# Weight sums of a Strassen down projection: 32 subtractions on GpSimd instead of VectorE

## The chip, the cores and the metric

The kernel runs on one NeuronCore of a Trainium2 chip. A core has a matrix engine (TensorE, PE in the profile; its weight loads are PEld) and three engines for elementwise work: VectorE (DVE), ScalarE (ACT) and GpSimd (POOL). SyncE (SP) only issues DMAs here. Each engine takes its instructions in its own order, and semaphores join them. The metric is the time of one execution on the device in microseconds, the median of several runs.

## The reference, cut to what matters

One decoder layer on 256 tokens (T = 256 in the kernel) with D = 1024 and a feed-forward width FF of 2816: a half-weighted feed-forward block, a mixer of two branches, and a second half-weighted feed-forward block. All numbers are float32.

```
def swiglu(x, w_gate, w_up, w_down):
    return (jax.nn.silu(x @ w_gate) * (x @ w_up)) @ w_down

h = h + 0.5 * rmsnorm(swiglu(rmsnorm(h, ffn1_pre_g[l]), ffn1_w_gate[l], ffn1_w_up[l], ffn1_w_down[l]), ffn1_post_g[l])
...
h = h + rmsnorm(merged @ w_out[l], mix_post_g[l])
h = h + 0.5 * rmsnorm(swiglu(rmsnorm(h, ffn2_pre_g[l]), ffn2_w_gate[l], ffn2_w_up[l], ffn2_w_down[l]), ffn2_post_g[l])
```

The change touches only `@ w_down`, in both feed-forward blocks, called f1 and f2 in the kernel.

## The kernel before

**Split weights.** A float32 product is made of three products of reduced-precision parts: high by high, low by high, high by low. So each piece of a weight that comes from DRAM (`raw`) is split into a high part by ScalarE (`whi`, `wqh`: a cast, L355, L132, L157) and a low part by VectorE (`wlo`, `wql`: the piece minus its high part, L356, L138, L158). TensorE can use a piece when both parts are there. A low part of 128x1024 elements reads two operands in SBUF.

**A feed-forward block.** Gate and up go in 11 chunks of 256 columns (j = 0 to 10; `pg_f` and `pup_f` are their results in PSUM, L437). ScalarE and VectorE evict them (L443, L444: VectorE reads one operand from PSUM), form the product `sg_f` (L1100) and split it into `gh_f` and `gl_f` (L416, L417). In the trace and below, chunk numbers count weight pieces: two to each j.

**Down by Strassen.** Four of the five 512-row groups of `w_down` are multiplied as Strassen quads: seven products in place of eight, each on a sum or a quarter of the weights. The plan `DOWN` is "q1 Q2 q3 Q0 ppp": quads 1 and 3 form their weight sums on the spot (`wt`, L124), quads 2 and 0 use sums that were made ahead and stand in DRAM (`sums_f`), and three plain pieces end the stage.

**The sums that are made ahead.** While gate and up run, `stored_sums` (L208 to L230) makes them, in four jobs per block: two halves (kt = 0, 1) of quad 2, then two of quad 0. A job loads two 128x1024 tiles of the weights (`ws`, L217), forms four differences of 128x512 in place (L222, L224, L227, L229), and stores each tile when it is ready (L225, L230). Loads and stores are DMAs that GpSimd issues. After its first load, GpSimd copies one element a partition of the tile (L219, `landed`), which keeps it from issuing more until that load has landed. SyncE loads the stored sums again in the down stage (`raw` from `sums_f`).

**What sets the order.** `store_sums` in the block's loop over j steps the jobs: the place in the program is written by hand. During gate and up a scheduler with a cost model arranges the instructions of each engine; from the down stage on the order is the written one. `ws`, `whi`, `wlo`, `wqh`, `wql`, `wt`, `gh_f` and `gl_f` take turns in one pool of 29 equal buffers (`k4`). A new tile gets the buffer that comes free first by that model, and its first writer waits until the last reader or writer of the old one is done. A `ws` buffer is free once its store has landed.

Of the kernel before, what the change touches and what calls it, by code (L numbers as in the profile page):

```python
# [56 lines left out]
def tile_hybrid_layer(ctx: ExitStack, tc: tile.TileContext, x, ffn1_pre_g, ffn1_w_gate, ffn1_w_up,  # L57
# [4 lines left out]
    nc = tc.nc  # L62
# [5 lines left out]
    def k4(shape, name, dt=F32):  # L68
        return sb.tile(shape, dt, tag="k4", name=name, bufs=K4_BUFS)
# [10 lines left out]
    def tiny(n, name):  # L80
        return sb.tile([P, n], F32, tag=f"tiny{n}", name=name, bufs=10 if n > 4 else 16)
# [129 lines left out]
    def stored_sums(w, k0, store, kt):  # L211

        t = []
        for i in range(2):
            t.append(k4([P, 2, 512], f"ws{k0}{kt}{i}"))
            rows = slice(k0 + (2 * i + kt) * P, k0 + (2 * i + kt + 1) * P)
            nc.gpsimd.dma_start(t[i], w[rows, :].rearrange("p (q c) -> p q c", q=2))  # L217
            if i == 0:
                nc.gpsimd.tensor_copy(tiny(2, f"landed{k0}{kt}")[:, 0:1], t[i][:, 0, 0:1])  # L219
            yield  # L220
        (q0, q1), (q2, q3) = ((x_[:, 0], x_[:, 1]) for x_ in t)
        nc.vector.tensor_sub(q0, q1, q0)  # L222
        yield
        nc.vector.tensor_sub(q1, q3, q1)  # L224
        nc.gpsimd.dma_start(store[:, 0, kt, :], t[0].rearrange("p q c -> p (q c)"))  # L225
        yield
        nc.vector.tensor_sub(q3, q3, q0)  # L227
        yield
        nc.vector.tensor_sub(q2, q2, q3)  # L229
        nc.gpsimd.dma_start(store[:, 1, kt, :], t[1].rearrange("p q c -> p (q c)"))  # L230
        yield

# [815 lines left out]
    def ffn(post_v, tag, ready, turned, then, products):  # L1048
# [29 lines left out]
        then()  # L1078
        sums = {}
        jobs = [stored_sums(*job) for job in stored.get(tag, ())]  # L1080

        def store_sums(at):
# [814 lines left out]
```

## Time and profile before

| | us |
|---|---|
| median of 3 runs | 725.26 (725.09 to 725.95) |
| profiled execution, first to last instruction (span) | 724.0 |
| weight sums on VectorE, busy | 22 (32 instructions) |
| GpSimd busy in the whole span | 57.5 |

The profile is one execution of its own, known by its span of 724.0 us; the runs also count what lies around the span, and their median is 1.26 us above it. In a row of the timeline stand the start, the duration, the engine, the line, the operation, the output and inputs, their shape, and in brackets how long the engine sat idle before it and what released it. A row "x3" joins three neighbours. In a row of groups stand the busy time, the mean in ns of one, and idle time ahead. A row of windows gives for a stretch of time its length and the busy time of PE, PEld, DVE, ACT and POOL, the granted clock, and the share and rate of the DMAs. Instructions of one engine overlap a little, so the step from start to start is shorter than the duration.

### The profile page before, as it was taken

To read this page: it belongs to the slowest core of one execution; us is meant where nothing else is said; L and a number is where in the kernel's file an instruction comes from. 1 tells how busy PE (TensorE), PEld (TensorE's weight loads), DVE (VectorE), ACT (ScalarE), POOL (GpSimd) and SP (SyncE) were. 2 spreads that over 40 slices of the span, in tenths; PEclk is the share of its full clock that TensorE was granted. 3 is DMA by queue.
4 is the path that set the end of the run, shared out by engine and by line. 5 is a ranking of instruction groups with operands and counts; after the bars stand their busy time and mean duration, and the time that the engine had idled before them with its cause. 6 is when DMAs were issued, how large, how long until landed. Compare 5 with 4: busy or idle time off the path is not lost.

```text
span 724.0 us, 10650 instructions
## 1 busy us (share of the span) xinstructions
PE 716.8 (99%) x3959; PEld 615.1 (85%) x3959; DVE 642.9 (89%) x993; ACT 487.1 (67%) x828; POOL 57.5 (8%) x103
## 2 busy tenths in 40 slices
PE   9999999999999999999999999999999999999996
PEld 7888898888878888899888788888888888888885
DVE  6889999999979999887996998789786899989996
ACT  5666666767767676879965577775664676577572
POOL 4401110000200000000000000000011021200000
PEclk9999999999999999999999999999999999999998
DMA  8969977877673657666564663464454868876851
GB/s 300 273 200 333 319 250 285 321 270 280 184 231 119 183 167 234 205 210 196 153 226 148 205 221 130 169 234 163 163 169 145 280 215 311 290 273 268 312 204 58
DMA packets 100213, 161.01 MB, mean 222 GB/s; under 512 B 3309, under 2 KB 69441, under 8 KB 99137
## 3 DMA queue, kind: packets, MB, share of 16 engines
q1 hardware_dynamic: 92880, 135.80, 56.7%
q0 software_dynamic: 6976, 24.00, 9.3%
q8 instruction: 31, 0.51, 0.3%
q10 hardware_dynamic: 304, 0.53, 0.2%
q14 instruction: 22, 0.17, 0.1%
HBM read 150.85 MB, written 9.47 MB: 221 GB/s over the span
## 4 chain that ended last, share of the span: by engine, by line
PE 99%; DVE 0%; DVEq 0%; ACT 0%; issue 0%; ACTq 0%
PE pup_f L437 14%; PE pg_f L437 14%; PE pxs L437 6%; PE pws L478 6%; PE pgt L478 6%; PE acc_f2p L934 5%; PE acc_f1p L934 5%; PE pbc L437 3%; PE pk L437 3%; PE pq L437 3%; PE pn_f L494 3%; PE pn_mx L478 3%; PE pwd L478 3%; PE pn_f L478 3%; PE pz L437 2%; PE acc_f1p L772 2%
## 5 line engine op out<-in xcount | busy, mean ns | idle before, releaser
L356 DVE TENSOR_TENSOR wlo<-raw,whi 128x1024 fp32r<-128x1024 f32 x204 | 243.5, 1221 | 17.1 <-ACT whi L355 16.6
L355 ACT CAST whi<-raw 128x1024 fp32r<-128x1024 f32 x204 | 206.9, 1050 | 11.1 <-DMA raw<-in_w_in_dram 4.0
L437 PE MATMUL pg_f<-u_f,whi 128*128 128x512 f32 x288 | 69.0, 390 | 0.0
L437 PE MATMUL pup_f<-u_f,whi 128*128 128x512 f32 x288 | 68.7, 391 | 0.0
L437 PEld LDWEIGHTS pg_f<-u_f,whi 128*128 128x128 f32 x288 | 53.9, 188 | 11.1
L437 PEld LDWEIGHTS pup_f<-u_f,whi 128*128 128x128 f32 x288 | 52.9, 188 | 10.2
L437 PEld LDWEIGHTS pg_f<-u_f,wlo 128*128 128x128 f32 x288 | 36.9, 191 | 1.4
L437 PE MATMUL pup_f<-u_f,wlo 128*128 128x256 f32 x288 | 37.5, 283 | 0.0
L437 PE MATMUL pg_f<-u_f,wlo 128*128 128x256 f32 x288 | 37.4, 283 | 0.0
L437 PEld LDWEIGHTS pup_f<-u_f,wlo 128*128 128x128 f32 x288 | 35.9, 192 | 0.0
L158 DVE TENSOR_TENSOR wql<-raw,wqh 128x1024 fp32r<-128x1024 f32 x28 | 32.9, 1222 | 0.9 <-ACT wqh L157 0.9
L478 PE MATMUL pgt<-whi,u_mx 128*128 128x512 f32 x128 | 33.1, 393 | 0.0
L416 ACT CAST gh_f<-sg_f 128x512 fp32r<-128x512 f32 x18 | 11.2, 621 | 30.3 <-DVE sg_f L1100 26.3
L437 PE MATMUL pxs<-u_mx,whi 128*128 128x512 f32 x128 | 29.9, 390 | 0.0
L443 ACT COPY su_f<-pup_f 128x256 f32<-128x256 f32 x36 | 13.4, 372 | 24.1 <-PE pup_f L437 24.1
L478 PEld LDWEIGHTS pgt<-whi,u_mx 128*128 128x128 f32 x128 | 23.6, 188 | 5.3 <-issue 0.7
L437 PEld LDWEIGHTS pxs<-u_mx,whi 128*128 128x128 f32 x128 | 23.8, 188 | 4.8
L157 ACT CAST wqh<-raw 128x1024 fp32r<-128x1024 f32 x28 | 27.4, 1048 | 0.0
L132 ACT CAST wqh<-wt 128x1024 fp32r<-128x1024 f32 x16 | 16.8, 1053 | 15.2 <-DVE wt L124 11.5
L1397 DVE SCALAR_TENSOR_TENSOR xs<-xr,cols_b,xs 128x255 f32<-128x255 f32 (+2 forms) x48 | 21.2, 480 | 0.8 <-ACT xs L1394 0.6
L1471 DVE TENSOR_TENSOR E<-E,cbm 128x768 f32<-128x768 f32 x16 | 15.3, 958 | 6.0 <-ACT E L511 6.0
L511 ACT ACTIVATE s<-s,nm 128x128 f32<-128x128 f32 (+1 forms) x32 | 14.3, 447 | 9.3 <-DVE nm L1564 7.2
(492 smaller groups left out, 1700.5 us busy)
## 6 DMA issues: line engine op xcount, KB each, us to landing
raw<-in_w_in_dram SPq DMA_DIRECT2D x40, 1024.0 KB, 5.2
raw<-in_ffn_w_gate_dram SPq DMA_DIRECT2D x20, 1024.0 KB, 5.8
raw<-in_ffn_w_up_dram SPq DMA_DIRECT2D x20, 1024.0 KB, 5.6
raw<-in_ffn_w_down_dram SPq DMA_DIRECT2D x18, 1024.0 KB, 5.3
ws<-in_ffn_w_down_dram POOLq DMA_DIRECT2D x16, 512.0 KB, 6.3
sums_f<-ws POOLq DMA_DIRECT2D x16, 512.0 KB, 5.5
raw<-sums_f SPq DMA_DIRECT2D x8, 1024.0 KB, 7.0
raw<-in_ssd_w_branch_dram SPq DMA_DIRECT2D x8, 1024.0 KB, 5.0
```

Of the source, the lines that this page charges most:

```text
L132: nc.scalar.copy(hi, src)
L157: nc.scalar.copy(hi, src)
L158: nc.vector.tensor_sub(lo, src, hi.bitcast(F32))
L355: last_cast[0] = behind(nc.scalar.copy(hi, r[:, js, :]), "cast").ins
L356: m = nc.vector.tensor_sub(lo, r[:, js, :], hi.bitcast(F32))
L437: nc.tensor.matmul(to, w_(j)[:, m * P:(m + 1) * P], x_(j), start=first and j == 0, stop=not first and j == KD - 1, skip_group_check=True)
L478: nc.tensor.matmul(acc, a(k0 + j), b(j), start=first and i == 0, stop=last and i == 11)
L494: nc.tensor.matmul(accs[b], x_(k0 + j), w_(j), start=first and j == 0 and w_ is wh and x_ is acts[b][0], stop=last and j == 3 and w_ is wl)
L772: nc.tensor.matmul(acc[b][q][:, cs] if to is None else to, x_[:, ts], w_(kt)[:, halves[q]][:, cs], start=to is not None and kt == 0 and x_ ...
L934: nc.tensor.matmul(bank[p], x_, w_, start=p not in begun, stop=last and p in (1, 5, 6, 7))
L1397: nc.vector.scalar_tensor_tensor(dst[:, m, s:], acc[:, m, :T - s], cw(3 - s, c), dst[:, m, s:], ALU.mult, ALU.add)
L1471: nc.vector.tensor_tensor(E, E, cbm[g].unsqueeze(1).to_broadcast([P, 2, 3 * P]), ALU.mult)
```

## The change

The four differences of a job are computed by GpSimd. Nothing else in the text of the kernel changes.

```
         (q0, q1), (q2, q3) = ((x_[:, 0], x_[:, 1]) for x_ in t)
-        nc.vector.tensor_sub(q0, q1, q0)
+        nc.gpsimd.tensor_sub(q0, q1, q0)
         yield
-        nc.vector.tensor_sub(q1, q3, q1)
+        nc.gpsimd.tensor_sub(q1, q3, q1)
         nc.gpsimd.dma_start(store[:, 0, kt, :], t[0].rearrange("p q c -> p (q c)"))
         yield
-        nc.vector.tensor_sub(q3, q3, q0)
+        nc.gpsimd.tensor_sub(q3, q3, q0)
         yield
-        nc.vector.tensor_sub(q2, q2, q3)
+        nc.gpsimd.tensor_sub(q2, q2, q3)
         nc.gpsimd.dma_start(store[:, 1, kt, :], t[1].rearrange("p q c -> p (q c)"))
```

TensorE and SyncE keep their instructions in the same order. GpSimd has 32 more (138 for 106), VectorE 32 fewer, and the scheduler arranges some others anew.

On GpSimd's queue, in gate and up of f1, this is the end of the first job and the begin of the second (`ws_448` and `ws_513` are the first job's tiles, `ws_630` and `ws_743` the second's; + stands only after the change, - only before):

```order
+L227 TENSOR_TENSOR ws_513<-ws_513,ws_448 128x512
+L229 TENSOR_TENSOR ws_513<-ws_513 128x512
+L230 DMA sums_f_66<-ws_513 128x1024
 L217 DMA ws_630<-in_ffn_w_down_dram 128x1024
 L219 COPY landed_632<-ws_630 128x1
-L230 DMA sums_f_66<-ws_513 128x1024
+L222 TENSOR_TENSOR ws_630<-ws_630 128x512
 L217 DMA ws_743<-in_ffn_w_down_dram 128x1024
+L224 TENSOR_TENSOR ws_630<-ws_743,ws_630 128x512
 L225 DMA sums_f_66<-ws_630 128x1024
```

The first load of the second job stood ahead of the first job's last store, and now stands behind it. The second load of a job now stands behind a subtraction.

On VectorE, at the end of gate and up of f1, these rows stood around the first low parts of quad 1 before (`wql221`, `wql222`, `wql223`; `ws011_1200` is the second tile of the last job; in brackets the semaphores that a row waits for, where DMAHW are loads by SyncE, DMASW DMAs by GpSimd, and Pool GpSimd's instructions):

```order
L138 TENSOR_TENSOR wql221_1310<-raw22_1155,wqh221_1308 128x1024 [waits DMAHW0_49]
L227 TENSOR_TENSOR ws011_1200<-ws011_1200,ws010_1087 128x512 [waits DVE_49]
L229 TENSOR_TENSOR ws011_1200<-ws011_1200 128x512 [waits DVE_49]
L444 TENSOR_TENSOR su_f19_1253<-pup_f191_1265,su_f19_1253 128x256 [waits Activation_49]
L138 TENSOR_TENSOR wql222_1314<-raw23_1211,wqh222_1312 128x1024 [waits DMAHW1_49]
L1100 TENSOR_TENSOR sg_f19_1202<-su_f19_1253,sg_f19_1202 128x512 [waits DVE_49]
L124 TENSOR_TENSOR wt225_1318<-raw22_1155 128x1024 [waits DMASW3_49]
L417 TENSOR_TENSOR gl_f18_1092<-sg_f19_1202,gh_f18_1091 128x512 [waits Activation_49]
L138 TENSOR_TENSOR wql223_1320<-raw23_1211,wqh223_1316 128x1024 [waits PE_49]
```

And after the change, at the same place:

```order
L138 TENSOR_TENSOR wql221_1310<-raw22_1155,wqh221_1308 128x1024 [waits DMAHW0_49,PE_49,Activation_49]
L444 TENSOR_TENSOR su_f19_1253<-pup_f190_1264,su_f19_1253 128x256 [waits Activation_49]
L138 TENSOR_TENSOR wql222_1314<-raw23_1211,wqh222_1312 128x1024 [waits DMASW3_49,DMASW1_49,DMAHW1_49,Activation_49,Pool_49]
L444 TENSOR_TENSOR su_f19_1253<-pup_f191_1265,su_f19_1253 128x256 [waits Activation_49]
L124 TENSOR_TENSOR wt225_1318<-raw22_1155 128x1024 [waits DMASW4_49,DMASW6_49,DMASW2_49,DMASW0_49]
L1100 TENSOR_TENSOR sg_f19_1202<-su_f19_1253,sg_f19_1202 128x512 [waits DVE_49]
L138 TENSOR_TENSOR wql223_1320<-raw23_1211,wqh223_1316 128x1024 [waits DMASW2_49,DMASW4_49,Activation_49,Pool_49]
```

The subtractions are gone from VectorE's order, `gl_f` has moved behind the third low part, and the buffers are dealt anew: `wql222` takes one that the last job's first tile held, `wql223` the one of its second tile, so they wait for that job's stores (L225 and L230). Before, neither of them waited for a DMA of GpSimd. The same rows stand in f2.

## The prediction

> **What bounds the kernel now.** I read the page first (busy time per engine, the granted clock, the chain that ended last), then the waits of TensorE, then the chain through the first feed-forward stage.
>
> ```profile
> PE 716.8 (99%) x3959; PEld 615.1 (85%) x3959; DVE 642.9 (89%) x993; ACT 487.1 (67%) x828; POOL 57.5 (8%) x103
> PEclk9999999999999999999999999999999999999998
> PE 99%; DVE 0%; DVEq 0%; ACT 0%; issue 0%; ACTq 0%
> PE warm L571 <- DVE zeros L551: 1.1, 1, 1.1
> 115.03 5.57 PE pup_f L437 x32
> 120.60 5.54 PE pg_f L437 x32
> ...
> 131.71 38.08 PE acc_f1p L934 x168
> ...
> 663.47 38.08 PE acc_f2p L934 x168
> ```
>
> TensorE is busy for 716.8 of 724.0 us at an undisturbed clock. Its only wait in the whole program is 1.1 us before its first instruction. In the chain each row begins where the one before ends: 115.03 + 5.57 is 120.60, and so on into the down stage at 131.71. The first part of the down stage takes 38.08 us in both FFNs. So TensorE sets the time from the first matmul to the last, and the end is a short tail behind it that the change does not touch. An engine that is relieved beside it gives TensorE nothing to gain; an engine that falls behind can cost one for one. The question is only whether the change makes something late.
>
> **What the change removes.** Thirty-two subtractions leave VectorE.
>
> ```profile
> L229 DVE TENSOR_TENSOR ws<-ws 128x512 f32<-128x512 f32 x8 | 5.5, 689 | 0.1
> L222 DVE TENSOR_TENSOR ws<-ws 128x512 f32<-128x512 f32 x8 | 5.5, 687 | 0.0
> L224 DVE TENSOR_TENSOR ws<-ws,ws 128x512 f32<-128x512 f32 x8 | 5.5, 686 | 0.0
> L227 DVE TENSOR_TENSOR ws<-ws,ws 128x512 f32<-128x512 f32 x8 | 5.5, 686 | 0.0
> ...
> 118.33 0.69 DVE L224 TENSOR_TENSOR ws<-ws,ws 128x512 f32<-128x512 f32 x1
> ...
> 120.70 0.69 DVE L227 TENSOR_TENSOR ws<-ws,ws 128x512 f32<-128x512 f32 x1
> 121.42 0.69 DVE L229 TENSOR_TENSOR ws<-ws 128x512 f32<-128x512 f32 x1
> 122.03 0.42 DVE L444 TENSOR_TENSOR su_f<-pup_f,su_f 128x256 f32<-128x256 f32 x1
> 122.37 1.22 DVE L138 TENSOR_TENSOR wql<-raw,wqh 128x1024 fp32r<-128x1024 f32 x1
> ...
> 125.84 1.23 DVE L138 TENSOR_TENSOR wql<-raw,wqh 128x1024 fp32r<-128x1024 f32 x1
> ```
>
> The groups sum to 4 x 5.5 = 22 us of busy time. Each holds VectorE's line for about 0.60 us, because neighbouring instructions overlap (121.42 to 122.03), so VectorE gains 32 x 0.60 = 19.2 us, half in each FFN. Three of these subtractions stand just ahead of the second and third low part (wql) of the first down quad, so those could come 1.8 us sooner. By the first part, none of this shortens TensorE's work: I count the relief at **0**, with at most 0.4 us for small stalls that the modelled ends of matmuls hide.
>
> **What it adds on GpSimd.** No subtraction of this size on GpSimd is in the trace. The nearest rows:
>
> ```profile
> L1308 POOL TENSOR_SCALAR_AFFINE_SELECT dneg<-dneg 128x256 f32<-128x256 f32 x1 | 0.4, 415 | 0.0
> L554 POOL TENSOR_SCALAR_AFFINE_SELECT ident<-ident 128x128 f32<-128x128 f32 x1 | 0.3, 285 | 0.0
> L219 POOL COPY landed<-ws 128x1 f32<-128x1 f32 x8 | 9.7, 1213 | 38.2 <-DMA ws<-in_ffn_w_down_dram 38.2
> ```
>
> From 128 to 256 elements the select grows by 415 - 285 = 130 ns, about 1.02 ns an element, over a base of 155 ns. With one pass over 512 elements that gives 0.155 + 512 x 1.02 ns = 0.68 us, the low end; with the two operands read one after the other, 0.155 + 1024 x 1.02 ns = 1.20 us, the high end. I take 1.2, since the subtraction reads two operands and no row shows GpSimd reading two at the price of one. Gain is excluded here, as nothing else goes from GpSimd.
>
> The Trainium skill, "GPSIMD Engine Reference", section 3.1, has a two-input add of 2048 fp32 elements at 4497 ns against 2293 ns on VectorE; scaled to 512 elements that would be an estimate of some 1.1 us, and the sum with it would be the same.
>
> **The job on GpSimd's queue.** The four subtractions of a job now stand between its DMAs, so a job runs one step after another. Two queue rows give the pieces, with the landing times of the DMA table:
>
> ```profile
> 25.12 0.53 POOL L217 DMA_DIRECT2D ws<-in_ffn_w_down_dram  x1
> 32.77 0.19 POOL L219 COPY landed<-ws 128x1 f32<-128x1 f32 x1 [7.12 <-DMA ws<-in_ffn_w_down_dram]
> ...
> 122.41 0.54 POOL L230 DMA_DIRECT2D sums_f<-ws  x1 [2.56 <-DVE ws L229]
> ...
> ws<-in_ffn_w_down_dram POOLq DMA_DIRECT2D x16, 512.0 KB, 6.3
> sums_f<-ws POOLq DMA_DIRECT2D x16, 512.0 KB, 5.5
> ```
>
> First load to landed 7.65, the copy 0.19, second load 6.3, two stores to issue 1.08: 15.2 us, and four subtractions of 1.2 make 20.0. Four jobs from 25.12 on would end at 105.1, without waits for VectorE. Each of the 20 reads by GpSimd (16 subtractions, 4 copies) can also wait for VectorE, as the copies do now: 1213 ns in the mean against 190 ns for the one that ran free, a wait of 1.02 us. Twenty waits between nothing and 1.02 are 0 to 20.4 us, so the last store goes out between 105 and 125.5 (122.41 before) and lands 5.5 later: 111 to 131, in the middle **121**. In the second FFN buffers hold the second job until 573.96; three jobs remain, with 15 reads:
>
> ```profile
> 573.96 0.53 POOL L217 DMA_DIRECT2D ws<-in_ffn_w_down_dram  x1 [11.50 <-PE pup_f L437]
> 657.69 1.22 DVE L138 TENSOR_TENSOR wql<-raw,wqh 128x1024 fp32r<-128x1024 f32 x1
> ```
>
> These give 573.96 + 60 + (0 to 15.3) + 5.5, thus 639 to 655, in the middle 647.
>
> **The new wait.** Through the shared pool of 29 buffers, the third low part of the first quad now takes the buffer of the last job's second tile: VectorE waits there until the last store has landed. Behind it stand all the other low parts and sums of that quad, and TensorE's down stage behind those. Before, that part began at 125.84 (657.69 in the second FFN). How late it may be is set further on:
>
> ```profile
> 119.00:173.00 54.00, 54.00 (x255) 45.37 (x254) 53.22 (x55) 37.68 (x45) 1.61 (x3) 1.00 0.79 282
> 170.06 3.49 DVE L356 TENSOR_TENSOR wlo<-raw,whi 128x1024 fp32r<-128x1024 f32 x3
> 172.80 0.39 PE L772 MATMUL acc_f1p<-wlo,gh_f 128*128 128x512 f32 x1
> ```
>
> VectorE is busy for 53.22 of the 54 us from 119 to 173. The second of the three low parts in the row runs from 171.19 (a step of 1.13 behind 170.06) to 172.41, and TensorE uses it at 172.80. So TensorE loses one for one what exceeds this 0.39 and the 0.78 that VectorE is idle on the way: a store may land as late as 125.84 + 1.2, about **127.0** (658.9 in the second FFN, taken over from the first). The middles hold this with 6 and 12 us to spare, and of the late ends only the first FFN's 131 exceeds it, by 4 us.
>
> Stores of earlier jobs are awaited too, by low parts of gate and up. The nearest in time: the second half of chunk 18 waits for the third job's first store. That job's first 16.5 us (7.65 + 0.19 + 1.2 + 6.3 + 1.2) follow two whole jobs, so it goes out at 25.12 + 40 + 16.5 = 81.7, at most 12.2 later with twelve waits, and lands by 99.5; the part began at 105.55. I count **0** there too.
>
> ```profile
> 105.55 1.22 DVE L356 TENSOR_TENSOR wlo<-raw,whi 128x1024 fp32r<-128x1024 f32 x1
> ```
>
> **The port between the two engines.** GpSimd's copy of one element a partition shows what it waits for:
>
> ```profile
> 589.57 4.30 POOL L219 COPY landed<-ws 128x1 f32<-128x1 f32 x1
> 589.93 1.23 DVE L356 TENSOR_TENSOR wlo<-raw,whi 128x1024 fp32r<-128x1024 f32 x1
> 591.06 0.43 DVE L838 TENSOR_TENSOR sv<-sg_f,sv 128x256 f32<-128x256 f32 x1
> 591.40 1.23 DVE L356 TENSOR_TENSOR wlo<-raw,whi 128x1024 fp32r<-128x1024 f32 x1
> 592.53 0.96 DVE L417 TENSOR_TENSOR sl<-sv,sh 128x768 fp32r<-128x768 f32 x1
> 593.40 0.43 DVE L417 TENSOR_TENSOR s<-sv,s 128x256 fp32r<-128x256 f32 x1
> 593.74 0.76 DVE L444 TENSOR_TENSOR sg_f<-pg_f,sg_f 128x256 f32<-128x256 f32 x2
> ```
>
> It was held for 4.30 us, across the ends of five VectorE instructions with two operands in SBUF, and ended at 593.87, just after VectorE began an eviction, which has one operand in PSUM. So GpSimd gets in where VectorE evicts or idles. A subtraction of 1.2 us that starts beside a pair of evictions (0.66 of line time) then keeps VectorE's next two-operand instruction waiting some 0.5 us, where 0.60 was saved: about nothing for VectorE, from a gain of 0.6 to a loss of 0.6 for each.
>
> The Trainium skill, "SBUF — State Buffer", section "Who interferes with whom", says that a VectorE instruction with two SBUF inputs contends with a GpSimd instruction that reads SBUF, and that whichever issues first holds the shared pair to its end. The row agrees that GpSimd is held, but over five instructions, which the rule alone does not say; what VectorE loses to a GpSimd instruction of 1.2 us no row here shows, and by this rule it would be the whole of it.
>
> **Sum.** Relief 0, TensorE unchanged, stores in time, some 0.3 us for VectorE's small stalls near the tight place: 724.0 + 0.3 = 724.3 for the profiled span. The median of the runs, 725.26, lies 1.26 above the span, so I forecast **725.6 us**. A difference under 0.2% (1.45 us) is about what cannot be told from no change.
>
> **The rivals.**
> *Late stores (slower).* The last store of the first FFN lands after 127.0, VectorE stands at the third low part of the first quad, and TensorE's down stage starves further on. The late end gives 131 - 127 = 4 us: 725.3 + 4, so about 729.3, and more if reads wait longer than the copies did (4.30 us is the longest). For it: a queue in which each step now waits for the one before. Against: six microseconds of margin in the middle, and a VectorE that is relieved. Chance 0.15.
> *VectorE is held by GpSimd (slower).* If GpSimd is let in at every instruction's end, each subtraction costs VectorE 1.2 and saves 0.60: 16 x 0.6 = 9.6 us in each FFN. Idle time in the gate and up stages takes part of it (8.6 us in the first, by this window), but not near the quads: at least the last job's 4 x 0.6 = 2.4, less the 0.4 of slack, so 2 to 5 us in each FFN, 4 to 10 in all; I take 6, so 731.3. It decides where a subtraction costs VectorE more than the 0.60 it saves by about 0.1 in the last job (0.39 over four).
>
> ```profile
> 24.00:131.50 107.50, 107.50 (x614) 94.61 (x613) 98.93 (x142) 67.81 (x105) 11.86 (x23) 1.00 0.82 271
> ```
>
> For it: VectorE is the second busiest engine. Against: the copy that waited 4.30 us. Chance 0.30.
> *Relief reaches TensorE (faster).* The waits of TensorE leave 0.4 us, so 724.9, which is inside no change; over 1.45 us would need waits that the trace does not have. Chance 0.05.
> *It does not do what it says.* If VectorE only waits where it subtracted, its busy time falls by 22 us and the time stays: this is inside no change.
>
> **How the numbers follow.** No change 0.50 (725.6, from 724.8 to 726.7), slower 0.15 + 0.30 = 0.45, faster 0.05. The range is 724.8 to 733.5: at the lower end the 0.4 us of relief, at the upper end 8.2 us over the median, which takes in the late stores at 4 and most of the hold's 4 to 10; what lies above is about 1 in 10, and as much lies below.
>
> **What would show it.** Right: subtractions on GpSimd of 0.7 to 1.2 us when free, the last store of the first FFN issued near 115, VectorE's busy time down by some 20, TensorE with one wait of 1.1 us, the down stage at 131.71 and 38.08 long. Late stores: VectorE idle ahead of wql with the releaser sums_f. A hold: wlo and evictions far above 1221 ns and 0.42 us, and gate or up rows longer than 5.57. What would make it wrong: a subtraction of 1.6 us or more when free, for four jobs would then end 16 x 0.4 = 6.4 us later and the margin of 6 us is gone.

## The result, and the profile after

| | before | after |
|---|---|---|
| median of 4 runs, us | 725.25 | 736.25 (735.02 to 737.44) |
| ratio of after to before | | 1.0144, 95% interval 1.0126 to 1.0161 |
| profiled execution, span, us | 724.0 | 735.7 |

The change makes the kernel 11.0 us slower. The forecast was no change, 725.6, and its range ended at 733.5.

The page of the kernel after, its busy times and the engines of the chain that ended last, then TensorE's waits (engine and line, what it waited for, us in total, times, longest):

```profile
PE 721.5 (98%) x3959; PEld 614.7 (84%) x3959; DVE 647.6 (88%) x961; ACT 484.7 (66%) x828; POOL 104.3 (14%) x135
...
PE acc_f1p L772 <- ACT whi L355: 1.9, 1, 1.9
PE acc_f2p L934 <- DVE wql L138: 1.7, 3, 0.6
PE acc_f1p L934 <- DVE wql L138: 1.6, 3, 0.6
PE pg_f L437 <- DVE sg_f L444: 1.2, 1, 1.2
PE warm L571 <- DVE zeros L551: 1.1, 1, 1.1
PE acc_f1p L772 <- DVE wlo L356: 0.5, 1, 0.5
PE acc_f1p L934 <- DVE wql L158: 0.2, 1, 0.2
```

Two things are to be seen. VectorE has 32 instructions fewer and is busy for longer: 647.6 us, against 642.9. And TensorE, which waited only before its first matmul, now waits 7.1 us more (1.9 + 1.7 + 1.6 + 1.2 + 0.5 + 0.2), while its busy time grows by 4.7 (721.5 - 716.8): matmuls with late weights are drawn apart, and behind the longest wait the granted clock was halved for 3.4 us. Together 11.8, which is the growth of the span, 11.7. Matmul by matmul the two traces give the places: 3.5 us in the quads of f1 (2.5 of them in the third), 4.6 at the last plain piece of f1, 1.7 in gate and up of f2 (nearly all at one gate piece), 2.6 in the third quad of f2, and 0.7 gained elsewhere.

The halved clock, as a row of windows, and two matmuls of that stretch, which are 0.42 us apart from start to start where 0.23 is usual:

```profile
179.50:182.90 3.40, 3.40 (x9) 2.63 (x9) 2.89 (x6) 0.59 (x1) 0.00 (x0) 0.50 0.70 201
...
180.05 0.63 PE L772 MATMUL acc_f1p<-whi,gl_f 128*128 128x512 f32 x1
180.47 0.63 PE L772 MATMUL acc_f1p<-wlo,gh_f 128*128 128x512 f32 x1
```

It makes up some 1.8 of the 4.6 us at the last plain piece; the waits there (1.9 and 0.5) are most of the rest.

The subtractions in GpSimd's groups (busy us, mean ns):

```profile
L229 POOL TENSOR_TENSOR ws<-ws 128x512 f32<-128x512 f32 x8 | 15.1, 1891 | 0.6
L224 POOL TENSOR_TENSOR ws<-ws,ws 128x512 f32<-128x512 f32 x8 | 12.9, 1607 | 31.9 <-DMA ws<-in_ffn_w_down_dram 31.9
L222 POOL TENSOR_TENSOR ws<-ws 128x512 f32<-128x512 f32 x8 | 11.6, 1449 | 0.7
L227 POOL TENSOR_TENSOR ws<-ws,ws 128x512 f32<-128x512 f32 x8 | 10.6, 1330 | 0.2
```

The shortest of them takes 1.29 us. The eight longest (2.15 to 2.35) each stand beside a low part that began before them, and end behind it: GpSimd waits for VectorE too.

What went wrong ahead of the first quad of f1 is seen in four timelines of the kernel after (start, duration, instruction, idle time before it and its releaser): VectorE, GpSimd, SyncE's queue, and ScalarE.

```profile
107.74 0.41 DVE L444 TENSOR_TENSOR sg_f<-pg_f,sg_f 128x256 f32<-128x256 f32 x1
108.07 4.24 DVE L356 TENSOR_TENSOR wlo<-raw,whi 128x1024 fp32r<-128x1024 f32 x2
112.23 0.74 DVE L444 TENSOR_TENSOR su_f<-pup_f,su_f 128x256 f32<-128x256 f32 x2
113.01 1.00 DVE L1100 TENSOR_TENSOR sg_f<-su_f,sg_f 128x512 f32<-128x512 f32 x1
...
107.70 1.29 POOL L224 TENSOR_TENSOR ws<-ws,ws 128x512 f32<-128x512 f32 x1 [3.26 <-DMA ws<-in_ffn_w_down_dram]
109.89 1.34 POOL L227 TENSOR_TENSOR ws<-ws,ws 128x512 f32<-128x512 f32 x1
111.31 2.16 POOL L229 TENSOR_TENSOR ws<-ws 128x512 f32<-128x512 f32 x1
113.76 0.58 POOL L230 DMA_DIRECT2D sums_f<-ws  x1 [0.30 <-POOL ws L229]
...
112.34 0.37 SPq L337 DMA_DIRECT2D raw<-in_ffn_w_down_dram  x1
118.10 0.37 SPq L337 DMA_DIRECT2D raw<-in_ffn_w_down_dram  x1
...
124.75 1.05 ACT L132 CAST wqh<-raw 128x1024 fp32r<-128x1024 f32 x1 [2.62 <-DMA raw<-in_ffn_w_down_dram]
...
125.89 1.22 DVE L138 TENSOR_TENSOR wql<-raw,wqh 128x1024 fp32r<-128x1024 f32 x1 [2.96 <-ACT wqh L132]
```

And the same loads and the same cast in the kernel before:

```profile
109.39 0.37 SPq L337 DMA_DIRECT2D raw<-in_ffn_w_down_dram  x1
115.39 0.37 SPq L337 DMA_DIRECT2D raw<-in_ffn_w_down_dram  x1
...
120.06 1.06 ACT L132 CAST wqh<-raw 128x1024 fp32r<-128x1024 f32 x1 [0.87 <-DMA raw<-in_ffn_w_down_dram]
```

Two low parts (wlo) that had taken 2.35 us together take 4.24: GpSimd's L224 begins at 107.70, before the first of them, and L227 at 109.89, just before the second. VectorE does most of a low part, which takes 1.22 us when free, after the subtraction is over: L227 ends at 111.23, the second low part at 112.31. The second low part is the last reader of a buffer for weight pieces, of which there are three. SyncE loads quad 1's first half when it comes free: at 112.34 instead of 109.39. Of these 2.95 us, 1.06 are lateness that VectorE had before the first of the two low parts, and 1.89 are the holds on them. The second half follows at 118.10 instead of 115.39 and lands at 124.73 (120.04 before): 2.71 us for the later issue, the rest for a slower landing (6.63 us for 4.65), which the run with fills below has too (6.35), without loss. So ScalarE's cast stands until 124.75, VectorE idles 2.96 us, and its second low part of the quad begins at 125.89 instead of 122.37, in a stage where VectorE has no time left. The last store, issued at 113.76, landed at 121.45 and is not what anyone waits for.

TensorE has time in hand at the first quad and pays later, where the low parts come closest to it, in the third. This is a low part of that quad and the first matmul that reads it, before and then after:

```profile
155.73 1.23 DVE L138 TENSOR_TENSOR wql<-wt,wqh 128x1024 fp32r<-128x1024 f32 x1
157.84 0.39 PE L934 MATMUL acc_f1p<-wql,sh 128*128 128x512 f32 x1
...
159.59 1.22 DVE L138 TENSOR_TENSOR wql<-wt,wqh 128x1024 fp32r<-128x1024 f32 x1
160.86 0.50 PE L934 MATMUL acc_f1p<-wql,sh 128*128 128x512 f32 x1 [0.62 <-DVE wql L138]
```

The low part is 3.86 us late and had been done 0.88 us ahead of its matmul. At the gate piece of f2 no load stands between: three VectorE instructions in a row from 597.51 on are held for 1.08, 1.49 and 0.48 us, and TensorE waits 1.2 us for an eviction behind them.

### The profile page after: what moved, and what is told of

Same layout as the page of the kernel before. It is cut to its first block, busy times and chain, and to the rows that moved or that the text cites. A ratio compares the mean times of both kernels' runs of the same rounds, so it can differ in the third digit from the quotient of the medians.

```text
span 735.7 us, 10672 instructions
## 1 busy us (share of the span) xinstructions
PE 721.5 (98%) x3959; PEld 614.7 (84%) x3959; DVE 647.6 (88%) x961; ACT 484.7 (66%) x828; POOL 104.3 (14%) x135
## 4 chain that ended last, share of the span: by engine, by line
PE 76%; DVE 12%; ACT 4%; issue 4%; DMA 3%; DVEq 0%; ACTq 0%
PE pg_f L437 7%; PE pup_f L437 7%; PE pxs L437 6%; PE pws L478 6%; PE pgt L478 6%; DVE wlo L356 5%; PE pbc L437 3%; PE pk L437 3%; PE pq L437 3%; PE pn_f L494 3%; PE pn_mx L478 3%; PE pwd L478 3%; DMA raw<-in_ffn_w_down_dram 3%; PE pn_f L478 3%; PE pz L437 2%
## 5 line engine op out<-in xcount | busy, mean ns | idle before, releaser
L356 DVE TENSOR_TENSOR wlo<-raw,whi 128x1024 fp32r<-128x1024 f32 x204 | 256.7, 1286 | 19.3 <-ACT whi L355 18.9
L158 DVE TENSOR_TENSOR wql<-raw,wqh 128x1024 fp32r<-128x1024 f32 x28 | 32.6, 1217 | 0.0
L157 ACT CAST wqh<-raw 128x1024 fp32r<-128x1024 f32 x28 | 27.4, 1048 | 0.0
L138 DVE TENSOR_TENSOR wql<-raw,wqh 128x1024 fp32r<-128x1024 f32 x15 | 18.1, 1217 | 7.0 <-ACT wqh L132 7.0
L132 ACT CAST wqh<-raw 128x1024 fp32r<-128x1024 f32 x15 | 15.3, 1048 | 8.1 <-DMA raw<-in_ffn_w_down_dram 8.0
```

Source lines behind the costliest of these rows:

```text
L132: nc.scalar.copy(hi, src)
L138: nc.vector.tensor_sub(lo, src, hi.bitcast(F32))
L157: nc.scalar.copy(hi, src)
L158: nc.vector.tensor_sub(lo, src, hi.bitcast(F32))
L356: m = nc.vector.tensor_sub(lo, r[:, js, :], hi.bitcast(F32))
```

## The experiments

Two theories stood at the start. **H**: GpSimd's subtractions hold VectorE, and its lateness costs TensorE. **B**: the new order that the scheduler made, and the buffers that now wait for stores, cost it. All times are medians; the kernel before had 725.37 on the first chip (24 runs), 725.38 on the second (14) and 725.63 on the third (7).

**GpSimd writes, and reads nothing.** Zeros in place of the differences:

```
-        nc.gpsimd.tensor_sub(q0, q1, q0)
+        nc.gpsimd.memset(t[0], 0.0)
-        nc.gpsimd.tensor_sub(q1, q3, q1)
+        nc.gpsimd.memset(t[1], 0.0)
```

(L227 and L229 as the second.)

> GpSimd fills the tiles with zeros (128x1024 each time) where it subtracted, so the sums for quads 2 and 0 are left out; the order on TensorE, ScalarE, VectorE and SyncE, the buffers and GpSimd's queue stay as in the changed kernel, and GpSimd still works about 1 us at each place but reads nothing from SBUF. Theory H (GpSimd's reads hold VectorE): 724.5 to 726.5, no stretched low parts, the loads of the first down pieces issued near 109.4 and 115.4 again. Theory B (the new order, and the buffers that wait for stores): 734 to 738, as after the change.

Measured: **725.58**, ratio 1.0003 (0.9993 to 1.0012). Its page, one of its groups of fills, and the timelines of VectorE and GpSimd at the place above:

```profile
PE 715.6 (99%) x3959; PEld 614.1 (85%) x3959; DVE 624.5 (86%) x961; ACT 486.9 (67%) x828; POOL 82.2 (11%) x135
...
L227 POOL MEMSET ws<- 128x1024 f32 x8 | 7.6, 955 | 0.5
...
106.66 2.35 DVE L356 TENSOR_TENSOR wlo<-raw,whi 128x1024 fp32r<-128x1024 f32 x2
...
107.31 0.96 POOL L224 MEMSET ws<- 128x1024 f32 x1 [2.93 <-DMA ws<-in_ffn_w_down_dram]
108.33 0.96 POOL L227 MEMSET ws<- 128x1024 f32 x1
```

GpSimd works beside the same two low parts, and they take 2.35 us again; SyncE's load goes out at 109.04. The trace has the same instructions in the same order as the changed kernel's on TensorE, ScalarE, VectorE and SyncE, so the order is not what costs: with nothing read by GpSimd, nothing is lost. The stores land sooner here, but in the changed kernel too they had landed (121.45 and 662.11, the last of f1 and f2) before the low parts that wait for them began (125.89 and 666.23). So B is out. VectorE's busy time is 624.5, so in the changed kernel 647.6 - 624.5 = 23.1 us are holds: 0.72 for each of 32 subtractions. In its trace 32 VectorE instructions beside a subtraction are longer than others of their form, one for each, by 0.28 to 1.49 us, 23.0 in all. In 31 of them the subtraction had begun first, and none is an eviction (L444), which has one operand in PSUM. A second profile of the changed kernel (further down) has VectorE busy for 650.0, thus 25.5 us of holds.

**No sums at all.**

```
-        nc.gpsimd.tensor_sub(q0, q1, q0)
+        pass
```

(all four lines)

> All 32 subtractions are left out, on both engines (the stored pieces are the weights themselves). What the relief of VectorE is worth alone: 724.6 to 725.6, as TensorE is the limit before.

Measured: **725.24** (median of 10 runs, some to 731.19; ratio 1.0019, 0.9998 to 1.0040). VectorE's busy time is 624.6. Freeing VectorE of the work altogether is worth nothing. Seven of the ten runs lie between 724.73 and 726.07 and three at 728.26, 729.42 and 731.19; no profile shows what they lost, but losses of this size come without any subtraction too.

**The last job, back on VectorE or alone on GpSimd.**

```
-        nc.gpsimd.tensor_sub(q0, q1, q0)
+        eng.tensor_sub(q0, q1, q0)
...
+        jobs = [stored_sums(*job, nc.vector if n == 3 else nc.gpsimd) for n, job in enumerate(stored.get(tag, ()))]
```

(with the engines exchanged in the second kernel)

> Only the last job of each block goes back to VectorE; twelve subtractions of a block stay on GpSimd. Theory H: the lateness ahead of the first quad goes away in both blocks, and with it what comes behind it; 1.5 us at a gate piece of the second block may stay: 725.5 to 729. If the twelve earlier subtractions make VectorE late as much, 732 to 736. Theory B: the buffers of the last job still wait for late stores, 733 to 737.

Measured: **728.69**, ratio 1.0054 (1.0034 to 1.0073).

> Only the last job of each block is on GpSimd, the other three on VectorE. Theory H with the tight place: most of the 11 us stays, 730 to 736. If lateness adds up over all four jobs: 726 to 729.

Measured: **731.06** (727.02 to 734.60), ratio 1.0071 (1.0045 to 1.0096). With the last job back, TensorE loses 0.2 us in the quads of the two blocks; what remains is 1.5 in gate and up of f2 and 2.6 at the last plain piece. With the last job alone it loses 3.2 in the quads, nothing in gate and up of f2, and again 2.6 at the last plain piece. By the medians 8 subtractions cost 5.7 us and the other 24 cost 3.3; the two intervals overlap, so which costs more is not shown, but for each subtraction the last job costs about five times as much (0.71 us against 0.14): the place matters more than the number. But three jobs of lateness add to it, since neither alone brings the load of quad 1 to 112.34: it goes out at 110.23 in the one and 110.33 in the other.

**One operand.** A copy in place of each subtraction:

```
-        nc.gpsimd.tensor_sub(q0, q1, q0)
+        nc.gpsimd.tensor_copy(q0, q1)
```

> GpSimd copies 128x512 elements where it subtracted (one operand in SBUF instead of two; the sums for quads 2 and 0 are left out); the order on the other engines and the buffers are those of the changed kernel. Theory H, with a hold as long as GpSimd's instruction: the copy takes about 0.7 us against 1.29, VectorE's busy time lies 10 to 14 us over that of the writes-only run (624.5) where the changed kernel lay 23 over it, and the time is 726 to 730. If only two-operand reads hold VectorE: 725 to 726 and busy time near 625.

Measured: **728.59**, ratio 1.0044 (1.0029 to 1.0059); VectorE's busy time 632.6, which is 8.1 over 624.5, less than the 10 to 14 expected. In the copy's timeline the hold can be seen:

```profile
106.78 2.76 DVE L356 TENSOR_TENSOR wlo<-raw,whi 128x1024 fp32r<-128x1024 f32 x2
109.47 0.74 DVE L444 TENSOR_TENSOR su_f<-pup_f,su_f 128x256 f32<-128x256 f32 x2
...
107.51 0.96 POOL L224 COPY ws<-ws 128x512 f32<-128x512 f32 x1 [2.99 <-DMA ws<-in_ffn_w_down_dram]
109.30 0.73 POOL L227 COPY ws<-ws 128x512 f32<-128x512 f32 x1
110.09 0.62 POOL L229 COPY ws<-ws 128x512 f32<-128x512 f32 x1
```

A free copy takes 0.62 us, about half of 1.29, and two low parts lose 0.41 instead of 1.89 (2.76 and 4.24, less 2.35). A one-operand read holds VectorE too, but for a shorter time.

**Subtractions in halves.**

```
-        nc.gpsimd.tensor_sub(q0, q1, q0)
+        for c in (slice(0, 256), slice(256, 512)):
+            nc.gpsimd.tensor_sub(q0[:, c], q1[:, c], q0[:, c])
```

> Each subtraction in two of 256 columns, so 64 shorter ones on GpSimd. Theory H: the hold lasts an instruction, and VectorE gets in between two; the sum of the holds stays (VectorE's busy time 20 to 28 over 624.5) and the time is 732 to 738. If it were the length of a single hold that matters (VectorE loses only what reaches beyond its next eviction): 727 to 731.

Measured: **729.88** (726.88 to 733.18), ratio 1.0066 (1.0043 to 1.0089); VectorE's busy time is 644.5, 20.0 over 624.5. The sum of the holds stays nearly the same, as H has it, but the time came out below its 732 to 738 and inside the 727 to 731 of the other reading, by which the length of a single hold matters. The order on the four other engines is that of the changed kernel. The two low parts at the tight place took 2.89 us, and quad 1's load went out at 110.63:

```profile
107.72 2.89 DVE L360 TENSOR_TENSOR wlo<-raw,whi 128x1024 fp32r<-128x1024 f32 x2
110.53 0.74 DVE L448 TENSOR_TENSOR su_f<-pup_f,su_f 128x256 f32<-128x256 f32 x2
111.31 1.14 DVE L1104 TENSOR_TENSOR sg_f<-su_f,sg_f 128x512 f32<-128x512 f32 x1
113.19 1.95 DVE L421 TENSOR_TENSOR gl_f<-sg_f,gh_f 128x512 fp32r<-128x512 f32 x1 [0.74 <-ACT gh_f L420]
```

Much of the same holding falls on instructions behind the one that gives the buffer back (1.14 for 0.69, 1.95 for 0.69). So the time does not follow the sum of the holds but where they fall.

**A fourth buffer for weight pieces.**

```
-K4_BUFS = 29
+K4_BUFS = 27
-RAW_BUFS = 3
+RAW_BUFS = 4
```

> The changed kernel with a fourth buffer for weight pieces (raw) and 27 instead of 29 shared buffers. If the lateness reaches TensorE through raw buffers given back late, and so loads issued late: at most 4 us over its control raw4_before. If VectorE's lateness reaches TensorE directly: 8 to 12 us over it.

Measured: **728.39**, ratio 1.0048 (1.0030 to 1.0066).

> The control for raw4: the kernel before with four raw and 27 shared buffers, no subtraction on GpSimd: 724 to 728.

Measured: **729.24**, ratio 1.0052 (1.0036 to 1.0069), above the expected 724 to 728. The page and TensorE's waits of raw4, the one with subtractions on GpSimd, and then two rows of its control:

```profile
PE 716.9 (99%) x3959; PEld 613.8 (85%) x3959; DVE 645.8 (89%) x961; ACT 484.0 (67%) x828; POOL 103.3 (14%) x135
...
PE warm L571 <- DVE zeros L551: 1.1, 1, 1.1
...
119.20 0.54 POOL L225 DMA_DIRECT2D sums_f<-ws  x1 [10.57 <-DVE ws L224]
...
128.57 1.23 DVE L138 TENSOR_TENSOR wql<-raw,wqh 128x1024 fp32r<-128x1024 f32 x1 [5.77 <-issue]
```

In raw4 VectorE is held as long as ever (645.8), and yet in the profiled execution, the fastest of its eight, TensorE waits only before its first matmul: quad 1's halves are loaded at 108.39 and 112.09, ahead of the need, and its second low part begins at 122.08, as early as in the kernel before. That fits a loss that passes through the weight buffers. It does not prove it, for the control is not clean. In the control that second low part stood until 128.57, just behind the landing (9.3 us after 119.20) of the last job's first store, and TensorE lost 4.9 us in the quads of f1, in a profile that is the slowest of its four runs. That looks like the loss that the prediction called late stores; raw4 does not have it, so the difference of the two is not the price of the change. Against the kernel before, raw4 is 3.0 us slower, and the scheduler has arranged it anew.

**The last plain piece of f1.** Its loss of 4.6 us did not follow the holds. In the trace its load landed 8.57 us after its issue, beside the load of a gain row (`pg_f`) that GpSimd issues at the same moment; before, 4.95. The changed kernel was run again, and once with that row loaded by SyncE behind it:

```
-        pg = load_gain(post_v, f"pg_{tag}")
+        pg = load_gain(post_v, f"pg_{tag}", nc.sync if tag == "f1" else nc.gpsimd)
```

> The changed kernel once more, unaltered, on the chip of gain_later. If the slow landing of the first block's last down piece (8.57 us after its issue, where 4.6 to 5.0 were measured without subtractions on GpSimd) belongs to the changed kernel, it lands after 8 us or more again and the time is 735 to 738; if it was chance, below 6 us and the time 731 to 734.

Measured: **734.75** (732.86 to 740.59), ratio 1.0141 (1.0097 to 1.0185).

> The changed kernel, with the first block's gain row (pg_f, 512 KB over all partitions) loaded by SyncE behind two pieces of w_in instead of by GpSimd at the same moment as the last down piece. If sharing the DMA engines with that load made the last down piece land late: it lands within 5.5 us, TensorE's loss at the end of the first block falls from 4.2 to under 1, and the time is 731 to 734 (the later gain may cost some of it). If not: it lands after 8 us, 735 to 738.

Measured: **740.72**, ratio 1.0206 (1.0166 to 1.0246). Neither expectation came out as a whole. In the profile of after_again, the same program, the load landed after 6.34 us and TensorE lost 0.7 there, but it lost 3.9 in the quads of f1, 1.5 in gate and up of f2, and 4.9 in the quads of f2. So the split by places varies from execution to execution, and so does the sum: the eight runs of this program lie between 732.86 and 740.59. In gain_later the piece landed after 4.74, as expected, and TensorE lost nothing there, but the time is above both ranges: the late row cost more (2.5 us of waiting for `h`), and gate pieces waited 3.1.

Sharing the DMA engines fits, but with the row beside it the landings were 4.60, 4.80, 4.95, 5.53, 6.34, 8.21, 8.27, 8.51 and 8.57 us in the nine profiles with three raw buffers. The four slow ones all have subtractions on GpSimd, none of which runs at that time. In these four the piece before had been slow too (7.4 to 7.6 us, against 5.1 to 7.0 in the other five) and was still landing 2.9 to 3.0 us after the last piece was issued (0.6 to 2.4 in the others). What makes them slow stays open. The halved clock behind the wait came in one of the four: in the profile of halves two waits of nearly the same length (1.78 and 0.53 us) left the clock at 1.00.

## Why the prediction was wrong

- **TensorE bounds the kernel, and relief is worth 0.** Right: without any sums 725.24. Its 0.4 us for stalls of TensorE and 0.3 for VectorE's come from no row, and no run shows them.
- **A subtraction takes 1.2 us when free.** Nearly: 1.29. Its working from the select's slope came near, with both operands read one after the other.
- **The last store of f1 goes out between 105 and 125.5, and lands in time.** Right: 113.76, landed at 121.45. The third low part began at 129.10, 2.1 us later than the 127.0 that the prediction allowed, but held up by other things. The new wait on stores, to which most of the working went, never bound in the changed kernel.
- **GpSimd gets in where VectorE evicts, and what VectorE then loses (about 0.5) is what it saves (0.60): "about nothing for VectorE".** This is the step that failed, in two ways. The size was 0.72 for each subtraction, within the 0 to 1.2 that the step allowed, so that VectorE is busy for 4.7 us more and not for about as long. GpSimd does not need an eviction to get in: it gets in ahead of a VectorE instruction that has not begun, also between two low parts (109.89 above), and then holds it, for 0.28 to 1.49 us over the 32 holds. The row on which the step rested, a copy held for 4.30 us, showed who waits when VectorE is first, and was read as a rule. And the two do not cancel because they do not fall at one place. Three of VectorE's own subtractions of the last job had stood at 118.33 to 121.42, behind the low part that gives the buffer back; GpSimd's run when their tile has landed, at 107.70 to 113.47, ahead of it and beside it. "TensorE unchanged" fell with this step: in the profile it lost 3.5 us in the quads of f1, 1.7 in gate and up of f2 and 2.6 in the quads of f2.
- **A delay of VectorE costs TensorE what exceeds the slack at the quads.** Too short a path. VectorE's end of a low part also starts the next load. The two loads of quad 1 went out 2.95 and 2.71 us late, the second landed 4.69 late (124.73 for 120.04), and VectorE's second low part began 3.5 late. The three raw buffers were not in the prediction at all. It also looked for the least slack at a plain piece (172.80), behind the quads; TensorE stood already in the second and third quad, where one low part had only 0.88 us to spare.
- **The rival in which VectorE is held by GpSimd** had the mechanism and 0.30 of the chance, and took 6 of a bound of 4 to 10; 11.0 was measured. Its "at least the last job's 4 x 0.6" was the right place. It had neither the reload nor the gate piece, but what they cost lies within its bound: without the 4.6 us at the last plain piece, whose cause is open, the profiled loss of 11.7 is 7.1. Of the signs that it named, the stretched low parts came; evictions were not held.

The Trainium skill, "SBUF — State Buffer", section "Who interferes with whom", was weighed as the rule that speaks against the change: whichever instruction issues first holds the shared pair to its end. The runs agree: in 31 of 32 holds the subtraction had begun first. Reads of one operand hold VectorE too (8.1 us in all, against 23.1 for two), and writes (0.96 us each) do not hold it at all, as the same section says.

## What to carry to other kernels

Work taken from a busy engine to an idle one is not removed if the two share a way to memory: count what the new engine holds (here 0.72 us against 0.60 saved) and where it falls, since it no longer stands where the old order had put it. An engine with slack for its consumer may have none for the load that its progress starts, so follow a delay through the buffers it gives back. A trial with the same instructions that only write tells contention from order and buffers in one run.

## What the runs showed of the hardware

A fill of 128x1024 by GpSimd (0.96 us) beside low parts of VectorE cost neither anything. A GpSimd subtraction of 128x512 took 1.29 us, about as long as two copies (0.62 each), and VectorE 0.69. Whichever of the two engines had begun first was as a rule the one that did not wait: GpSimd in 31 of the 32 holds, VectorE beside the eight longest subtractions. Split into two, the holds on VectorE summed to nearly the same: 20.0 us for 64 against 23.1 for 32. The landing of one 1 MB load, issued at the same point of the program, varied from 4.6 to 8.6 us between profiles. Behind waits of 1.85 and 0.53 us TensorE's granted clock was 0.50 for 3.4 us in one profile; behind waits of 1.78 and 0.53 it stayed at 1.00 in another.
